# A float32 transformer kernel: the gate and up products of its four SwiGLU layers by seven block products instead of eight, with the down products cut into groups

## The chip, the cores and the metric

The kernel runs on one core of one Trainium2 chip. The metric is the device time of one execution in microseconds (us), the median of several runs. One profiled execution gives the start, duration and engine of every instruction: PE (TensorE, the matmuls; PEld are its weight loads), DVE (VectorE), ACT (ScalarE), POOL (GpSimd), SP (which issues DMAs).

## The reference, cut to what matters

S = 512 tokens, D = 1024 features, D_FF = 2816. Two layers of a first block, each with a SwiGLU before and one after four attention mixers, then a second block that the change doesn't touch.

```python
def swiglu(h, w_gate, w_up, w_down):
    return (jax.nn.silu(h @ w_gate) * (h @ w_up)) @ w_down

for l in range(DEPTH):                                   # DEPTH = 2
    x = x + 0.5 * swiglu(rms_norm(x, ffn1_norm[l]), ffn1_w_gate[l], ffn1_w_up[l], ffn1_w_down[l])
    ...
    x = x + jnp.concatenate([ya, yb, yc, yd], axis=-1) @ w_out[l]
    x = x + 0.5 * swiglu(rms_norm(x, ffn2_norm[l]), ffn2_w_gate[l], ffn2_w_up[l], ffn2_w_down[l])
    x = rms_norm(x, final_norm[l])
```

## The kernel before, in words

Activations lie feature-major: x[k] is a tile of 128 features by 512 tokens, k = 0 to 7. A float32 product is made of three TensorE passes over float32r pairs: each operand is split into a high part (an ACT copy) and a low part (a DVE subtraction), and `mm3` (L98 to L102) multiplies high by high, high by low and low by high. The split activations are xh[k] and xl[k]; the split weights whi and wlo, of which three pairs exist at a time (`weights_`), fed by a DMA into raw, an ACT copy (L89) and a DVE subtraction (L90).

`ffn` is called four times: FFN1 and FFN2 of layer 0, then of layer 1. FFN2 of layer 0 is followed by FFN1 of layer 1 directly; elsewhere the mixers, or the second block, come between. The norm's per-token scale is not in xh and xl: it is a broadcast tile R (`bcast`, L127 and L130), which multiplies the finished gate and up sums, so that the products can begin before the scale is known. `late` (L219 to L222) multiplies x itself by such a scale after FFN2 of layer 0.

`ffn` works in two halves of 11 tiles f, a tile being 128 of the 2816 hidden features. For each f the gate product goes to a PSUM bank s and the up product to a bank t, each 8 k-tiles by three passes = 24 matmuls of 512 columns. Then a = s*R (L245), silu, u = t*R (L249), u*s (L250), and the split of the result into gh[f] and gl[f]. After 11 tiles the half's down products follow: for each of 8 output tiles k, 33 matmuls of 512 columns from gh and gl into a bank acc, then x[k] += 0.5*acc (L270). In the second half done(k) follows each k: `emit_h` makes xh[k] and xl[k] of the next stage (L181, L182) and, by an ACT square (L194) and a POOL addition (L199), the running sum of squares of the next norm.

Each engine runs its instructions in the order the tile scheduler has set; the weights are pulled 100 instructions ahead (`ahead`).

## Time and profile before

| | |
|---|---|
| time, median of 3 runs | 2573.12 us (2571.47 to 2574.28) |
| span of the profiled execution | 2570.1 us |
| PE busy | 2491.1 us, 97%, 12456 matmuls |
| DVE busy | 1353.0 us, 53% |
| ACT busy | 1054.0 us, 41% |
| POOL busy | 517.6 us, 20% |

The profiled execution's own time is its span, 3 us under the median; nothing outside the span is in the records. The four FFNs take 8 to 377, 702 to 1073, 1073 to 1441 and 1767 to 2136 us of it. A matmul's record lasts longer than its distance to the next one, since matmuls are pipelined, so what one matmul costs is the distance from start to start.

### The profile page before, as it was taken

The numbers are of one execution on the slowest core, as the hardware profiler recorded it, in microseconds if no ns is written. First come the engines' busy times: TensorE is split into PE (matmuls) and PEld (weight loads), VectorE is DVE, ScalarE is ACT, GpSimd is POOL, SyncE is SP. The second block draws the span as 40 slices with busy tenths as digits, with TensorE's granted clock in tenths as the row PEclk, the third lists the DMA queues.
The fourth block names the chain that finished last, engine by engine and source line by source line (L and its number), as shares of the span: only waits on it lengthen the run. The fifth ranks groups of instructions, "written<-read, shape, count | busy, mean of one in ns | idle before, by whom it ended". The sixth has DMA issues, their size and how long they took to land.

```text
span 2570.1 us, 32068 instructions
## 1 busy us (share of the span) xinstructions
PE 2491.1 (97%) x12456; PEld 2044.5 (80%) x12456; DVE 1353.0 (53%) x2259; ACT 1054.0 (41%) x1826; POOL 517.6 (20%) x431
## 2 busy tenths in 40 slices
PE   8999999899999999999999999999999999889998
PEld 6888888776688888888888988767888888768867
DVE  6434446976544344454344489755434444854444
ACT  4223236676522233332233476754322334343543
POOL 1000015652200000200000457223000014442312
PEclk9999999999999999999999999999999999989979
DMA  4233243211222322322333332012333334220111
GB/s 154 92 97 99 87 139 100 89 46 38 65 91 86 103 99 86 102 92 86 103 99 102 117 97 81 19 53 84 98 88 103 97 107 134 62 66 30 36 46 56
DMA packets 86137, 220.04 MB, mean 86 GB/s; under 512 B 19088, under 2 KB 22225, under 8 KB 85985
## 3 DMA queue, kind: packets, MB, share of 16 engines
q1 hardware_dynamic: 82576, 217.66, 27.1%
q8 instruction: 98, 1.61, 0.3%
q10 hardware_dynamic: 3408, 0.33, 0.1%
q14 instruction: 55, 0.44, 0.1%
HBM read 209.14 MB, written 8.78 MB: 85 GB/s over the span
## 4 chain that ended last, share of the span: by engine, by line
PE 86%; DVE 10%; ACT 2%; issue 1%; DMA 1%; POOL 0%; SPq 0%; DVEq 0%; POOLq 0%; ACTq 0%
PE acc L100 9%; PE acc L101 9%; PE acc L102 9%; PE s L101 7%; PE s L102 7%; PE s L100 7%; PE t L102 6%; PE t L101 6%; PE t L100 6%; PE acc L314 4%; PE t L461 2%; PE s L421 2%; PE t L514 2%; PE acc L1598 2%; DVE p L434 1%
## 5 line engine op out<-in xcount | busy, mean ns | idle before, releaser
L89 ACT ACTIVATE whi<-raw 128x1024 fp32r<-128x1024 f32 (+4 forms) x415 | 395.2, 953 | 1071.5 <-PE acc L101 349.6
L90 DVE TENSOR_TENSOR wlo<-raw,whi 128x1024 fp32r<-128x1024 f32 (+3 forms) x341 | 369.6, 1084 | 205.3 <-ACT whi L89 204.6
L199 POOL TENSOR_TENSOR sq<-sq,sqt 128x512 f32<-128x512 f32 x59 | 83.4, 1422 | 1395.8 <-issue 1233.6
L100 PE MATMUL s<-xh,whi 128*128 128x512 f32 x736 | 289.1, 393 | 8.5 <-ACT whi L89 8.0
L101 PE MATMUL s<-xl,whi 128*128 128x512 f32 x736 | 289.2, 393 | 5.5 <-DVE xl L182 5.3
L102 PE MATMUL s<-xh,wlo 128*128 128x512 f32 x736 | 287.9, 391 | 0.0
L101 PE MATMUL acc<-gl,whi 128*128 128x512 f32 x704 | 278.1, 395 | 0.0
L102 PE MATMUL acc<-gh,wlo 128*128 128x512 f32 x704 | 278.1, 395 | 0.0
L100 PE MATMUL acc<-gh,whi 128*128 128x512 f32 x704 | 276.8, 395 | 0.0
L101 PE MATMUL t<-xl,whi 128*128 128x512 f32 x704 | 275.0, 391 | 0.0
L100 PE MATMUL t<-xh,whi 128*128 128x512 f32 x704 | 274.6, 390 | 0.0
L102 PE MATMUL t<-xh,wlo 128*128 128x512 f32 x704 | 274.6, 390 | 0.0
L90 POOL TENSOR_TENSOR wlo<-raw,whi 128x1024 fp32r<-128x1024 f32 (+2 forms) x74 | 169.0, 2285 | 204.1 <-ACT whi L89 195.2
L249 DVE TENSOR_TENSOR u<-t,R 128x512 f32<-128x512 f32 x88 | 60.8, 691 | 275.5 <-PE t L102 275.5
L100 PEld LDWEIGHTS s<-xh,whi 128*128 128x128 f32 x736 | 139.2, 189 | 38.1 <-ACT whi L89 8.0
L101 PEld LDWEIGHTS s<-xl,whi 128*128 128x128 f32 x736 | 139.1, 189 | 38.1 <-DVE xl L182 9.6
L314 PE MATMUL acc<-whi,xh 128*128 128x256 f32 (+1 forms) x576 | 167.0, 293 | 2.1 <-DVE gate L1012 1.7
L314 PE MATMUL acc<-wlo,xh 128*128 128x256 f32 (+1 forms) x576 | 168.1, 293 | 0.3 <-DVE wlo L90 0.3
L314 PE MATMUL acc<-whi,xl 128*128 128x256 f32 (+1 forms) x576 | 168.2, 293 | 0.0
L102 PEld LDWEIGHTS s<-xh,wlo 128*128 128x128 f32 x736 | 139.0, 189 | 29.4 <-DVE wlo L90 0.8
L102 PEld LDWEIGHTS acc<-gh,wlo 128*128 128x128 f32 x704 | 132.0, 187 | 32.4
L101 PEld LDWEIGHTS acc<-gl,whi 128*128 128x128 f32 x704 | 131.9, 187 | 32.4
(662 smaller groups left out, 4750.7 us busy)
## 6 DMA issues: line engine op xcount, KB each, us to landing
raw<-in_ffn_gu_dram SPq DMA_DIRECT2D x176, 512.0 KB, 3.4
raw<-in_ffn_d_dram SPq DMA_DIRECT2D x64, 384.0 KB, 3.1
raw<-in_ffn_d_dram SPq DMA_DIRECT2D x64, 320.0 KB, 2.9
raw<-in_w2f_dram SPq DMA_DIRECT2D x25, 512.0 KB, 3.3
xs<-x SPq DMA_DIRECT2D x24, 256.0 KB, 2.0
raw<-in_a_dram SPq DMA_DIRECT2D x12, 512.0 KB, 3.5
x<-xs SPq DMA_DIRECT2D x24, 256.0 KB, 2.9
raw<-in_wo_dram SPq DMA_DIRECT2D x10, 512.0 KB, 4.0
```

The costliest lines, as they stand in the source:

```text
L89: nc.scalar.activation(out=hi, in_=raw, func=AF.Copy)
L90: (lo_eng or self.lo_eng).tensor_tensor(out=lo, in0=raw, in1=hi.bitcast(F32), op=ALU.subtract)
L100: mm(out=out, lhsT=lh, rhs=rh, start=start, stop=False)
L101: mm(out=out, lhsT=lh, rhs=rl, start=False, stop=False)
L102: mm(out=out, lhsT=ll, rhs=rh, start=False, stop=stop)
L199: nc.gpsimd.tensor_tensor(out=acc, in0=acc, in1=q, op=ALU.add)
L249: nc.vector.tensor_tensor(out=u, in0=prods[1], in1=R, op=ALU.mult)
L314: mm = lambda l, r, st=False, sp=False: nc.tensor.matmul(out=ps[i], lhsT=l, rhs=r, start=st, stop=sp, skip_group_check=True)
L421: nc.tensor.matmul(out=o, lhsT=q[:, i * P:(i + 1) * P], rhs=k[:, keys], start=(n == 0), stop=(n == len(pairs) - 1))
L461: nc.tensor.matmul(out=ps[r, a:z], lhsT=v[:, j, c0:c0 + 64], rhs=pts[j][:, a:z], start=(m == 0), stop=(m == n - 1), skip_group_check=True)
L514: nc.tensor.transpose(ps[:, i * P:(i + 1) * P], probs[i][:, o:o + P], b.ident)
L1598: mm = lambda i, l, r, st=False: nc.tensor.matmul(out=ps[i], lhsT=l, rhs=r, start=st, stop=False, skip_group_check=True)
```

## The change: seven block products, and down products in groups

Tiles f = 0 to 2 (`DIRECT = 3`) are made as before (`direct`). For f = 3 to 21 gate and up together are taken as one product of blocks: the weights as [[gate k 0-3, gate k 4-7], [up k 0-3, up k 4-7]], the activations as [[k 0-3, tokens 0-255 and 256-511], [k 4-7, the same]], and Winograd's form of Strassen's method makes it with seven block products where there are eight. Each block product is 4 k-tiles by three passes = 12 matmuls of 256 columns, so a tile takes 84 matmuls of 256 columns instead of 48 of 512.

The activations' seven forms are made once per FFN by `forms`, from x, the norm's gain and R, so they wait for R: for each of 4 k, two scale operations on DVE, four subtractions of 256 columns on POOL, four ACT copies and four DVE subtractions give fh[k] and fl[k]. They stand behind tile f = 0 in the program. The weights' forms are made for each f by `blocks`: four DMAs of 256 KB into the slots of xh and xl (which are free once the direct tiles are done; the tile f = 3 borrows slots of gh and gl), two sums on POOL and two on DVE of 128x512, seven ACT copies and seven DVE subtractions into four whi/wlo pairs. `winograd` runs the products and joins them with one ACT copy and five DVE additions of 256 columns. The multiplications by R (two of 128x512) and the split of 128x1024 weights fall away for these tiles.

The down products are cut into groups of 4, 4, 4, 4, 3 and 3 tiles f (`CHUNKS`). Those of one group are issued among the next group's gate and up, two k at a time (three in part of the groups of three); x[k] is updated 6 times per FFN. Only the last group of three tiles leaves its eight down products of 9 matmuls, with done(k), at the end of the FFN. In FFN2 of layer 1 the last update goes through a temporary tile and an ACT copy. 

```diff
-HALF = NFF // 2
...
+    def direct(self, gp, wgu, f, R):
+        nc = self.nc
+        prods = []
+        for which in range(2):
+            wh, wl = self.weights(wgu[f, which], (KT, P))
+            ps = self.bank("st"[which], 3)
+            for k in range(KT):
+                self.mm3(ps, wh[:, k], wl[:, k], self.xh[k], self.xl[k], k == 0, k == KT - 1)
+            prods.append(ps)
+        s = self.t(gp, "s")
+        nc.vector.tensor_tensor(out=s, in0=prods[0], in1=R, op=ALU.mult)
+        nc.scalar.activation(out=s, in_=s, func=AF.Silu)
+        u = self.t(gp, "cu")
+        nc.vector.tensor_tensor(out=u, in0=prods[1], in1=R, op=ALU.mult)
+        return u, s
+    def forms(self, gp, gain, R):
+        nc = self.nc
+        out = []
+        for k in range(4):
+            hs = []
+            for j, tag in ((k, "gh3"), (k + 4, "gl3")):
+                h = self.t(gp, tag)
+                nc.vector.scalar_tensor_tensor(out=h, in0=self.x[j], scalar=gain[:, j:j + 1], in1=R, op0=ALU.mult, op1=ALU.mult)
+                hs.append(h)
+            a, b = hs
+            H, L = self.t(gp, f"fh{k}", (P, 7, 256), F32R), self.t(gp, f"fl{k}", (P, 7, 256), F32R)
+            half = lambda t: t.rearrange("p (e c) -> p e c", e=2)
+            w0, w1 = half(self.t(gp, "cu")), half(self.t(gp, "s"))
+            lo, hi = slice(0, 256), slice(256, 512)
+            sub = lambda o, x, y: nc.gpsimd.tensor_tensor(out=o, in0=x, in1=y, op=ALU.subtract)
+            sub(w0[:, 0], a[:, hi], a[:, lo])
+            sub(w0[:, 1], b[:, hi], w0[:, 0])
+            sub(w1[:, 0], b[:, hi], a[:, hi])
+            sub(w1[:, 1], b[:, lo], w0[:, 1])
+            for j, src in ((0, half(a)[:, 0:1]), (1, half(b)), (3, w0), (5, w1)):
+                n = src.shape[1]
+                nc.scalar.activation(out=H[:, j:j + n], in_=src, func=AF.Copy)
+                nc.vector.tensor_tensor(out=L[:, j:j + n], in0=src, in1=H[:, j:j + n].bitcast(F32), op=ALU.subtract)
+            out.append((H, L))
+        return out
+    def blocks(self, gp, wgu, f):
+        nc = self.nc
+        with self.tc.high_priority(offset=self.ahead):
+            if f == DIRECT:
+                slots = [(gp, f"g{t}{4 + i}") for t in "hl" for i in range(4)]
+            else:
+                slots = [(self.xp, f"x{t}{4 * (f % 2) + i}") for t in "hl" for i in range(4)]
+            slot = iter(slots)
+            A = []
+            for which in range(2):
+                for e in range(2):
+                    t = self.t(*next(slot))
+                    nc.sync.dma_start(out=t, in_=wgu[f, which][:, e * S:(e + 1) * S])
+                    A.append(t)
+            a11, a12, a21, a22 = A
+            s1, s2, s3, s4 = (self.t(*next(slot)) for _ in range(4))
+            for eng, o, x, y, op in ((nc.gpsimd, s1, a21, a22, ALU.add), (nc.vector, s2, s1, a11, ALU.subtract),
+                                     (nc.gpsimd, s3, a11, a21, ALU.subtract), (nc.vector, s4, a12, s2, ALU.subtract)):
+                eng.tensor_tensor(out=o, in0=x, in1=y, op=op)
+            out = []
+            for pair in ((a11, s2), (s1, s3), (a12, s4), (a22,)):
+                hi = self.wp.tile([P, 1024], F32R, tag="whi", name=self.name("whi"), bufs=3)
+                lo = self.wp.tile([P, 1024], F32R, tag="wlo", name=self.name("wlo"), bufs=3)
+                for e, src in enumerate(pair):
+                    c = slice(e * S, (e + 1) * S)
+                    nc.scalar.activation(out=hi[:, c], in_=src, func=AF.Copy)
+                    nc.vector.tensor_tensor(out=lo[:, c], in0=src, in1=hi[:, c].bitcast(F32), op=ALU.subtract)
+                    v = lambda t: t[:, c].rearrange("p (k m) -> p k m", k=4)
+                    out.append((v(hi), v(lo)))
+        return out
+    def winograd(self, gp, wgu, f, F):
+        nc = self.nc
+        a11, s2, s1, s3, a12, s4, a22 = self.blocks(gp, wgu, f)
+        pa, pb = self.bank("s", 3), self.bank("t", 3)
+        lo, hi = slice(0, 256), slice(256, 512)
+        def prod(out, w, j, start=False, stop=False):
+            wh, wl = w
+            for k in range(4):
+                H, L = F[k]
+                for n, (x, y) in enumerate(((wh, H), (wh, L), (wl, H))):
+                    nc.tensor.matmul(out=out, lhsT=x[:, k], rhs=y[:, j], start=start and k == 0 and n == 0, stop=stop and k == 3 and n == 2,
+                                     skip_group_check=True)
+        add = lambda o, x, y: nc.vector.tensor_tensor(out=o, in0=x, in1=y, op=ALU.add)
+        prod(pa[:, lo], a11, 0, start=True)
+        prod(pa[:, hi], s2, 4)
+        t, U2, V = (self.t(gp, n, (P, 256)) for n in ("w6", "wu", "wv"))
+        u, s = self.t(gp, "cu"), self.t(gp, "s")
+        nc.scalar.activation(out=t, in_=pa[:, hi], func=AF.Copy)
+        add(U2, pa[:, lo], t)
+        prod(pb[:, lo], s1, 3, start=True)
+        prod(pb[:, hi], s3, 5)
+        add(V, pb[:, lo], U2)
+        add(u[:, hi], pb[:, hi], V)
+        prod(pa[:, lo], a12, 1, stop=True)
+        nc.scalar.activation(out=s[:, lo], in_=pa[:, lo], func=AF.Silu)
+        prod(pb[:, lo], s4, 2)
+        add(s[:, hi], pb[:, lo], U2)
+        nc.scalar.activation(out=s[:, hi], in_=s[:, hi], func=AF.Silu)
+        prod(pb[:, hi], a22, 6, stop=True)
+        add(u[:, lo], pb[:, hi], U2)
+        return u, s
+    def ffn(self, r, wgu, wd, gain, done, reorder=False):
         nc = self.nc
         with self.tc.tile_pool(name=self.name("ffn"), bufs=1, reuse_waits="tile") as gp:
             R = self.bcast(r, gp, "R", ACC)
-            self.late()
-            for half in range(2):
-                gh, gl = [], []
-                for f in range(HALF):
-                    prods = []
-                    for which in range(2):
-                        wh, wl = self.weights(wgu[half * HALF + f, which], (KT, P))
-                        ps = self.bank("st"[which], 3)
-                        for k in range(KT):
-                            self.mm3(ps, wh[:, k], wl[:, k], self.xh[k], self.xl[k], k == 0, k == KT - 1)
-                        prods.append(ps)
-                    a = self.t(gp, "a")
-                    nc.vector.tensor_tensor(out=a, in0=prods[0], in1=R, op=ALU.mult)
-                    s = self.t(gp, "s")
-                    nc.scalar.activation(out=s, in_=a, func=AF.Silu)
-                    u = self.t(gp, "u")
-                    nc.vector.tensor_tensor(out=u, in0=prods[1], in1=R, op=ALU.mult)
-                    nc.vector.tensor_tensor(out=u, in0=u, in1=s, op=ALU.mult)
-                    h = self.t(gp, f"gh{f}", dt=F32R)
-                    l = self.t(gp, f"gl{f}", dt=F32R)
-                    nc.scalar.activation(out=h, in_=u, func=AF.Copy)
-                    nc.vector.tensor_tensor(out=l, in0=u, in1=h.bitcast(F32), op=ALU.subtract)
-                    gh.append(h)
-                    gl.append(l)
-                if half == 1:
-                    self.new_h()
-                for k in range(KT):
-                    ps = self.bank("acc", 2)
-                    for f0, f1 in ((0, 6), (6, HALF)):
-                        wh, wl = self.weights(wd[half, k][:, f0 * P:f1 * P], (f1 - f0, P))
-                        for f in range(f0, f1):
-                            self.mm3(ps, wh[:, f - f0], wl[:, f - f0], gh[f], gl[f], f == 0, f == HALF - 1)
-                    old, new = self.x[k], self.x[k]
-                    if reorder:
-                        new = self.x[k] = self.t(gp, f"xa{k}") if half == 0 else self.t(self.xp, f"x{k}")
-                    v = (lambda a: a.rearrange("p (c r) -> p r c", r=8)) if reorder and half else (lambda a: a)
-                    o = new.rearrange("p (r c) -> p r c", r=8) if reorder and half else new
-                    nc.vector.scalar_tensor_tensor(out=o, in0=v(ps), scalar=0.5, in1=v(old), op0=ALU.mult, op1=ALU.add)
-                    if half == 1:
-                        done(k)
+            F = None
+            def up(f, i):
+                u, s = self.direct(gp, wgu, f, R) if f < DIRECT else self.winograd(gp, wgu, f, F)
+                nc.vector.tensor_tensor(out=u, in0=u, in1=s, op=ALU.mult)
+                h = self.t(gp, f"gh{i}", dt=F32R)
+                l = self.t(gp, f"gl{i}", dt=F32R)
+                nc.scalar.activation(out=h, in_=u, func=AF.Copy)
+                nc.vector.tensor_tensor(out=l, in0=u, in1=h.bitcast(F32), op=ALU.subtract)
+                return h, l
+            def down(k, f0, f1, g):
+                ps = self.bank("acc", 2)
+                wh, wl = self.weights(wd[k][:, f0 * P:f1 * P], (f1 - f0, P))
+                for j, (h, l) in enumerate(g):
+                    self.mm3(ps, wh[:, j], wl[:, j], h, l, j == 0, j == f1 - f0 - 1)
+                x = self.x[k]
+                if reorder and f1 == NFF:
+                    t = self.t(gp, "R" if k % 2 else "xa")
+                    v = lambda a: a.rearrange("p (c r) -> p r c", r=8)
+                    nc.vector.scalar_tensor_tensor(out=t.rearrange("p (r c) -> p r c", r=8), in0=v(ps), scalar=0.5, in1=v(x), op0=ALU.mult, op1=ALU.add)
+                    nc.scalar.activation(out=x, in_=t, func=AF.Copy)
+                else:
+                    nc.vector.scalar_tensor_tensor(out=x, in0=ps, scalar=0.5, in1=x, op0=ALU.mult, op1=ALU.add)
+            downs = []
+            for n, (f0, f1) in enumerate(zip(CHUNKS, CHUNKS[1:])):
+                g = []
+                for f in range(f0, f1):
+                    g.append(up(f, 4 * (n % 2) + f - f0))
+                    if F is None:
+                        F = self.forms(gp, gain, R)
+                        self.late()
+                    for _ in range(-(-len(downs) // (f1 - f))):
+                        downs.pop(0)()
+                downs = [lambda k=k, f0=f0, f1=f1, g=g: down(k, f0, f1, g) for k in range(KT)]
+            self.new_h()
+            for k in range(KT):
+                downs[k]()
+                done(k)
+CHUNKS = (0, 4, 8, 12, 16, 19, NFF)
+DIRECT = 3
...
-        b.ffn(r, A[f"ffn1_gu{l}"], A[f"ffn1_d{l}"], done_mix)
+        b.ffn(r, A[f"ffn1_gu{l}"], A[f"ffn1_d{l}"], g["ffn1_g", 0] if l == 0 else g["next", 0], done_mix)
-        b.ffn(r, A[f"ffn2_gu{l}"], A[f"ffn2_d{l}"], lambda k: b.emit_h(k, gn, g["fin_g", l]), l == 1)
+        b.ffn(r, A[f"ffn2_gu{l}"], A[f"ffn2_d{l}"], g["ffn2_g", l], lambda k: b.emit_h(k, gn, g["fin_g", l]), l == 1)
...
-            w[f + "_d"] = np.stack([feat_units(d[:HALF * P]), feat_units(d[HALF * P:])], 0)
+            w[f + "_d"] = feat_units(d)
```

How instructions move, at three places.

TensorE in the first FFN, from the last pass of tile f = 2 to tile f = 3; s and t are PSUM banks, fh0 and fl0 the forms of k = 0, whi and wlo the weights. Before:

```order
L102 MATMUL t_87_394<-xh7_31_143,wlo_86_391 128x512
L100 MATMUL s_96_436<-xh0_3_81,whi_94_432 128x512
L101 MATMUL s_96_436<-xl0_4_82,whi_94_432 128x512
L102 MATMUL s_96_436<-xh0_3_81,wlo_95_433 128x512
L100 MATMUL s_96_436<-xh1_7_89,whi_94_432 128x512
```

After:

```order
L101 MATMUL t_109_472<-xh7_31_143,wlo_108_469 128x512
L317 MATMUL s_130_545<-fh0_68_287,whi_122_523 128x256
L317 MATMUL s_130_545<-fl0_69_288,whi_122_523 128x256
L317 MATMUL s_130_545<-fh0_68_287,wlo_123_524 128x256
L317 MATMUL t_131_546<-fh0_68_287,whi_124_529 128x256
L317 MATMUL s_130_545<-fh1_74_307,whi_122_523 128x256
```

Where tile f = 3 needed only what the stage before had left, xh and xl, it now needs the forms, which R and a chain on DVE, POOL and ACT precede. In the first FFN 52 direct matmuls stand behind the broadcast of R on this engine, in the others 84, 66 and 84.

GpSimd in the first FFN, behind the norm's scale rs4. Before, nothing of the FFN's inside runs there, and the next norm's sums follow:

```order
L119 TENSOR_TENSOR rs4_50_199<-ms_49_197,neghalf_72 128x4
L199 TENSOR_TENSOR sq_405_2244<-sq_405_2244,sqt_415_2298 128x512
L199 TENSOR_TENSOR sq_405_2244<-sq_405_2244,sqt_425_2353 128x512
L199 TENSOR_TENSOR sq_405_2244<-sq_405_2244,sqt_435_2408 128x512
L199 TENSOR_TENSOR sq_405_2244<-sq_405_2244,sqt_445_2463 128x512
```

After, from the last subtraction of the forms of k = 1 on; xl2, xl0, xl6 and xl4 are block sums for f = 4 and f = 5, cu and s hold the forms of k = 2 and 3:

```order
L260 TENSOR_TENSOR s_77_310<-gl3_73_305,cu_76_309 128x256
L292 TENSOR_TENSOR xl2_145_659<-xh0_139_649,xh2_141_653 128x512
L292 TENSOR_TENSOR xl0_143_657<-xh2_141_653,xh3_142_655 128x512
L260 TENSOR_TENSOR cu_82_329<-gh3_78_323 128x256
L292 TENSOR_TENSOR xl6_178_841<-xh4_172_831,xh6_174_835 128x512
L260 TENSOR_TENSOR s_83_330<-gl3_79_325,gh3_78_323 128x256
L292 TENSOR_TENSOR xl4_176_839<-xh6_174_835,xh7_175_837 128x512
L260 TENSOR_TENSOR cu_82_329<-gl3_79_325,cu_82_329 128x256
L260 TENSOR_TENSOR cu_88_349<-gh3_84_343 128x256
L260 TENSOR_TENSOR s_83_330<-gl3_79_325,cu_82_329 128x256
L260 TENSOR_TENSOR cu_88_349<-gl3_85_345,cu_88_349 128x256
L260 TENSOR_TENSOR s_89_350<-gl3_85_345,gh3_84_343 128x256
```

Four block sums, whose inputs are loaded into slots that the direct tiles still read, now stand ahead of seven of the eight subtractions for k = 2 and 3.

VectorE in a steady tile of the first FFN. Before, tile f = 5; a and u are the gate and up sums, R the broadcast scale:

```order
L245 TENSOR_TENSOR a_127_638<-s_122_582,R_53_209 128x512
L90 TENSOR_TENSOR wlo_138_683<-raw_136_680,whi_137_682 128x1024
L249 TENSOR_TENSOR u_129_642<-t_126_613,R_53_209 128x512
L250 TENSOR_TENSOR u_129_642<-u_129_642,s_128_640 128x512
L90 TENSOR_TENSOR wlo_147_725<-raw_145_722,whi_146_724 128x1024
L254 TENSOR_TENSOR gl5_131_646<-u_129_642,gh5_130_645 128x512
```

After, twelve rows in tile f = 7, from its first addition on; xl5 and xl7 are block sums, x6 a residual tile that takes a down product:

```order
L320 TENSOR_TENSOR wu_257_1260<-s_254_1233,w6_256_1259 128x256
L320 TENSOR_TENSOR wv_258_1261<-t_255_1234,wu_257_1260 128x256
L320 TENSOR_TENSOR cu_259_1262<-t_255_1234,wv_258_1261 128x256
L89 TENSOR_TENSOR wlo_266_1341<-raw_264_1338,whi_265_1340 128x512
L292 TENSOR_TENSOR xl5_309_1568<-xl4_308_1567,xh4_304_1559 128x512
L292 TENSOR_TENSOR xl7_311_1570<-xh5_305_1561,xl5_309_1568 128x512
L320 TENSOR_TENSOR s_260_1263<-t_255_1234,wu_257_1260 128x256
L89 TENSOR_TENSOR wlo_270_1361<-raw_268_1358,whi_269_1360 128x512
L370 SCALAR_TENSOR_TENSOR x6_26_132<-acc_263_1337,x6_26_132 128x512
L300 TENSOR_TENSOR wlo_280_1394<-xh0_271_1377,whi_279_1393 128x512
L300 TENSOR_TENSOR wlo_280_1394<-xl1_276_1386,whi_279_1393 128x512
L320 TENSOR_TENSOR cu_259_1262<-t_255_1234,wu_257_1260 128x256
```

Six rows per tile became twenty, and the block sums, the weights' splits and the additions that drain PSUM stand in one row on this engine.

## Rows read from the trace of the kernel before

**Rows 1.** The page: busy time, the chain by engine, a group with mean ns.
```profile
PE 2491.1 (97%) x12456; PEld 2044.5 (80%) x12456; DVE 1353.0 (53%) x2259; ACT 1054.0 (41%) x1826; POOL 517.6 (20%) x431
...
PE 86%; DVE 10%; ACT 2%; issue 1%; DMA 1%; POOL 0%; SPq 0%; DVEq 0%; POOLq 0%; ACTq 0%
...
L89 ACT ACTIVATE whi<-raw 128x1024 fp32r<-128x1024 f32 (+4 forms) x415 | 395.2, 953 | 1071.5 <-PE acc L101 349.6
```
**Rows 2.** Stretches of two FFNs: PE, PEld, DVE, ACT, POOL busy, clock, DMA share, GB/s.
```profile
135.00:377.00 242.00, 242.00 (x1054) 197.33 (x1053) 100.71 (x122) 70.57 (x91) 8.58 (x6) 1.00 0.33 104
...
1092.00:1260.00 168.00, 168.00 (x735) 137.56 (x734) 75.90 (x96) 46.29 (x58) 0.00 (x0) 1.00 0.31 93
```
**Rows 3.** Timeline of PE, 200 to 240 us: first and last of 178 gate/up matmuls.
```profile
199.72 0.39 PE L100 MATMUL s<-xh,whi 128*128 128x512 f32 x1
...
239.84 0.39 PE L100 MATMUL s<-xh,whi 128*128 128x512 f32 x1
```
**Rows 4.** Timeline of PE, 320 to 360 us: first and last of 173 down matmuls.
```profile
319.76 0.40 PE L101 MATMUL acc<-gl,whi 128*128 128x512 f32 x1
...
359.89 0.40 PE L102 MATMUL acc<-gh,wlo 128*128 128x512 f32 x1
```
**Rows 5.** The chain of waits: start, us; two runs of 256-column matmuls (L314, stationary xh).
```profile
377.09 6.12 PE acc L314 x51
...
384.10 16.93 PE acc L314 x141
```
**Rows 6.** Timeline of PE and DVE, FFN2 of layer 0: its first matmul, and R's copy.
```profile
702.54 0.50 PE L100 MATMUL s<-xh,whi 128*128 128x512 f32 x1 [0.24 <-ACT xh L181]
...
723.95 0.69 DVE L130 COPY R<-acc 128x512 f32<-128x512 f32 x1 [0.61 <-PE acc L127]
```
**Rows 7.** Timeline of DVE, 1091 to 1100 us: back-to-back operations of 128x512.
```profile
1091.44 0.69 DVE L245 TENSOR_TENSOR a<-s,R 128x512 f32<-128x512 f32 x1
1092.04 0.68 DVE L249 TENSOR_TENSOR u<-t,R 128x512 f32<-128x512 f32 x1
...
1093.84 5.39 DVE L221 SCALAR_TENSOR_TENSOR x<-x,fin_g,sqt 128x512 f32<-128x512 f32 x8
```
**Rows 8.** Groups by line with busy us, mean ns: POOL at 256 and 512 columns.
```profile
L199 POOL TENSOR_TENSOR sq<-sq,sqt 128x512 f32<-128x512 f32 x59 | 83.4, 1422 | 1395.8 <-issue 1233.6 <-ACT sqt L194 161.8
...
L362 POOL TENSOR_TENSOR dup<-x,ahr 128x256 f32<-128x256 f32 x32 | 20.5, 672 | 69.8 <-PE t L390 69.8
```
**Rows 9.** The page's DMA issues: KB each, us from issue to landing.
```profile
x<-xs SPq DMA_DIRECT2D x24, 256.0 KB, 2.9
```
**Rows 10.** Timeline of PE, 702 to 713 us: a stall, and the two matmuls' distance behind it.
```profile
705.89 0.80 PE L101 MATMUL s<-xl,whi 128*128 128x512 f32 x1 [2.62 <-DVE xl L182]
706.49 0.63 PE L102 MATMUL s<-xh,wlo 128*128 128x512 f32 x1
...
711.18 0.63 PE L100 MATMUL s<-xh,whi 128*128 128x512 f32 x1
711.61 0.49 PE L101 MATMUL s<-xl,whi 128*128 128x512 f32 x1
```
**Rows 11.** Timeline of DVE and POOL, end of FFN2 of layer 0, from one down product's drain.
```profile
1057.59 0.69 DVE L270 SCALAR_TENSOR_TENSOR x<-acc,x 128x512 f32<-128x512 f32 x1 [2.13 <-PE acc L102]
1059.16 0.74 DVE L182 SCALAR_TENSOR_TENSOR xl<-x,gnext,xh 128x512 fp32r<-128x512 f32 x1
...
1059.64 2.68 POOL L199 TENSOR_TENSOR sq<-sq,sqt 128x512 f32<-128x512 f32 x2 [5.03 <-ACT sqt L194]
...
1065.29 0.69 DVE L270 SCALAR_TENSOR_TENSOR x<-acc,x 128x512 f32<-128x512 f32 x1 [2.13 <-PE acc L102]
```
**Rows 12.** Timeline of DVE and POOL at the kernel's start, both busy side by side.
```profile
10.15 9.86 POOL L199 TENSOR_TENSOR sq<-sq,sqt 128x512 f32<-128x512 f32 x6 [9.71 <-ACT sqt L194]
10.31 10.27 DVE L182 SCALAR_TENSOR_TENSOR xl<-x,ffn_g,xh 128x512 fp32r<-128x512 f32 x6
```

More of the change, by code (lines that the diff above doesn't have):

```diff
@@ L58, in load @@
         return t
-    BUFS = dict(sqt=2, ms=4, hms=4, rs4=4, rs8=2, r12=2, a=2, s=2, u=2, nm=6, sum=6, rsum=6, cms=2, lms=2, lats=2,
+    BUFS = dict(sqt=2, ms=4, hms=4, rs4=4, rs8=2, r12=2, s=2, cu=2, wu=2, nm=6, sum=6, rsum=6, cms=2, lms=2, lats=2,
                 beta=2, sq_=1, st=10, p=8, pth=3, ptl=3, vv=2, lat=6, ysq=2, c1=4, sums=3, frs=2, ft=2, fR=2, rr=1, y=4, dup=4, bias=1,
@@ L225, in post_norm @@
         return r
-    def ffn(self, r, wgu, wd, done, reorder=False):
+    def direct(self, gp, wgu, f, R):
[13 more added lines that the diff above has]
+        return u, s
```

## The prediction

> **What bounds the kernel now.** The page first: PE is busy 97% of the span and the chain that ends last is 86% PE, with DVE next at 53% busy [rows 1]. Then the FFN stretches, where all of the change lies: PE is busy for every one of the 242 and 168 us shown, at full clock, DVE for 42 to 45%, POOL hardly or not at all [rows 2]. So the FFNs are bound by PE alone, and a matmul saved there is time saved until another engine's chain takes over. Then the distance from start to start: 0.2267 us for a gate or up matmul (40.12 us over 177 steps) [rows 3] and 0.2333 for a down matmul (40.13 over 172) [rows 4]. For 256 columns the trace has the runs of the mixers' L314: 6.12 us over 51 and 16.93 over 141, both 0.1200 [rows 5].
>
> **The gate and up products.** A tile costs 48 x 0.2267 = 10.88 us now. After, it costs 84 matmuls of 256 columns, 21,504 columns in place of 24,576, but with 84 starts in place of 48. Their price lies between two rows. L314's 0.1200 [rows 5] gives 10.08 us, a gain of 0.80 per tile. But at 512 columns the trace has two prices for the same shape, and what differs is the moving tile: xh and xl at 0.2267, gh and gl, which lie in the FFN's own pool, at 0.2333, a step of 0.0067. The forms fh and fl lie in that same pool, so I add the step: 0.1200 + 0.0067 = 0.1267, 10.64 us, a gain of 0.24 per tile. There are 4 x 19 = 76 such tiles: 18 us by 0.1267, 61 us by 0.1200. I take **18**, as gh is nearer to fh in where it lies. The down products stay 528 of 512 columns per FFN, from gh and gl: 0.
>
> A Trainium skill page speaks for more: "TensorE: Matmul & The Clock Gate" (section "Wait — 56ns, not 53.3ns?") gives a warm matmul N / 2.4 GHz plus about 2.5 ns from start to start. That is 215.8 ns at 512 columns and 109.2 at 256, and by it the gain would be, as an estimate, 48 x 0.2158 - 84 x 0.1092 = 1.19 us per tile, 90 us in all. The trace disagrees: 0.2267 and 0.1200 are each about 13 ns over N / 2.4 [rows 3, 5].
>
> **The forms.** Before, R is needed only to drain the banks. Now it starts a chain that the fourth tile waits for. In FFN2 of layer 0 R is copied 21.4 us after the first product [rows 6], while the three direct tiles last 144 x 0.2267 = 32.6 us. In the built order 52, 84, 66 and 84 direct matmuls stand behind the broadcast of R in the four FFNs: 11.8, 19.0, 15.0 and 19.0 us of cover. From R to the last fl DVE has 40, 41, 49 and 41 instructions. Back to back they start 0.60 us apart, the scale operations with two tensors and a column 0.66 (L221: eight in 5.39) [rows 7]. Each list has 8 scale operations (16 in FFN1 of layer 1, where `late` adds 8) and 4 additions of 256 columns, put at half; with one 1024-column split in the FFN2s that is 23.4, 24.5, 29.3 and 24.5 us. Less the cover: 11.6, 5.5, 14.3 and 5.5, together 37. A low end: some 34 block-product matmuls of k = 0 and 1 can run in each FFN while the rest arrives, 34 x 0.1267 = 4.3 us, so 20 in all. I credit no such filling, because in the FFN1s POOL stands in the way. There the sums for f = 4 and 5 stand ahead of seven subtractions for k = 2 and 3, and their loads wait until the direct tiles have read xh and xl: after the last direct matmul come a DMA of 2.9 us [rows 9], two sums of 1.42 and seven subtractions of 0.67 [rows 8], 10.4 us, which agrees with 11.6 and 14.3 and no less. A high end: if DVE waits out every POOL operation that runs meanwhile, 16 x 0.67 + 4 x 1.42 = 16.4 us more per FFN, of which some is idle already; I put 61 for the four.
>
> Each stall also costs clock. After a stall of 2.62 us TensorE's matmuls start 0.43 us apart, the 1.2 GHz level, from 706.49 to 711.61: 12 steps at 0.427 where 0.2267 would do, 2.4 us [rows 10]. Four stalls: 9. Forms in all: 37 + 9 = **46**, ends 20 and 70.
>
> **The tails.** The last half's eight downs took 7.70 us each (1057.59 to 1065.29) [rows 11], 33 matmuls, which hid everything that done(k) does. Now they are 9 matmuls, 9 x 0.2333 = 2.10 us. Per k POOL has 2.68 us [rows 11], so the sum of squares ends about 8 x (2.68 - 2.10) = 4.6 us later against PE than it did, and R with it. DVE has 0.69 for x and 0.74 for xl [rows 11] and about 0.6 for a weight split, 2.0 us, just under 2.10; but beside a busy POOL six xl took 10.27 us, 1.71 each [rows 12], which makes it 3.0 and 0.9 late per k. The next stage takes its k in order at 0.68 each (three passes), so it feels between nothing and 4 us. Four FFNs: 0 to 16, I take **8**. The copy through ACT in the last FFN hides behind those same matmuls.
>
> **Steady tiles (f = 5 on).** PE needs 84 x 0.1267 + 24 x 0.2333 = 16.2 us per tile. DVE has 20 instructions, at 0.60 at most 12.0. ACT has 13, at the 0.953 of mostly larger copies [rows 1] at most 12.4. POOL has two sums, 2.84. All are under 16.2, so PE keeps the end, but the orders are tight: whi and wlo have three buffers for six weights per tile, so the next tile's first pair waits for this tile's seventh product, with only 10 down matmuls, 2.3 us, to cover one ACT copy and one DVE subtraction (1.2 us) and whatever those two engines have in hand. Before, no such wait shows [rows 2]. Bounds: nothing, or the 0.7 us of one operation in hand at each of 68 tiles, 48. I take one in eight, about 5, and 1 us for the last group in each FFN, where the gl of tile 21 is late for its own down products: **9**.
>
> **Sum.** 2570.1 - 18 + 46 + 8 + 9 = 2615 for a profiled execution. The median stood 3 us above the span, so **2618**.
>
> **Rivals.** (1) The cheap matmul: the 0.0067 step is not the pool's, and the block products run at L314's 0.1200. For it: the only row at 256 columns. Against: gh. It gives 43 us back: 2575, and this is the case on the other side, faster once the other terms stay under 56 us where I have 63. (2) The forms are hidden: the scheduler's cover holds, R comes early, and the low end of 20 minus the clock decides; 2618 - 37 = 2581 at 0.1267, and 2538 with the cheap matmul. Against: R at 21.4 us of 32.6. (3) POOL locks DVE in every tile. In rows 12 a DVE operation with two SBUF inputs, 0.74 alone [rows 11], lasts as long as the POOL operation beside it. In a steady tile POOL's 2.84 us, each sum of which can hold such a DVE operation, would come on top of 12.0, and both sums head the chain of the weight splits; if 0.6 us per tile then shows on PE, 76 x 0.6 = 46: 2664.
>
> The Trainium skill, "SBUF — State Buffer" (section "Who interferes with whom"), has this as an exclusive lock on a port pair that DVE and GpSimd share. The pairs of rows 12 agree with it, 1.71 us against 0.74.
>
> (4) The price goes by columns alone: half of 0.2267 for 256, 0.1133. Then a tile costs 9.52 us, the gain is 1.36 per tile, 103 in all: 2533. Against: L314's 0.1200 [rows 5]; no row of this kernel shows it.
>
> The page named above comes nearest to that; by its own 90 us the sum would be 2546.
>
> **Chances.** My own sum 0.50, the cheap matmul 0.24, hidden forms 0.10, the lock 0.13, a price by columns alone 0.03. My sum's own range, by the bounds of its terms, is 2592 to 2650. Eight in ten must leave out the cheapest combination (cheap matmul with hidden forms) and the far end of the lock: 2552 to 2662. About 0.2%, 5 us, is what a measurement of this kernel can tell from no change. Faster: half of the cheap matmul, half of the hidden forms, and the price by columns: 0.20. Within: a third of the cheap matmul: 0.08. Slower: the rest, 0.72.
>
> **What would show it.** In the profile after: the distance from start to start of L317 matmuls in a steady tile (0.1267, or 0.1200); an idle gap on PE ahead of L317 at the start of f = 3 in each FFN, with DVE fl or ACT fh as its releaser, 5 to 15 us, and half clock behind it; PE busy without gaps from f = 5 on, with 16.2 us per tile (15.7 in rival 1); POOL's L260 rows of k = 2 and 3 starting after the direct tiles' end in the FFN1s; DVE's subtractions L300 at 0.69 (over 1.2 beside L292 if the lock rules). The prediction is wrong if PE has no gap at f = 3, or gaps in every tile.

## The result, and the profile after

The changed kernel takes 2590.04 us (median of 5 runs, 2586.50 to 2595.99) against 2571.47 (5 runs, 2561.88 to 2574.28). The ratio on record is 1.0102, 95% interval 1.0073 to 1.0131, which is 26 us; the two medians by themselves are 19 us apart (1.0072), and the profiled execution spans 2588.3 us, 18 more than before's. So the change is slower, as forecast, by 18 to 26 us instead of the forecast 45 (from 2573), and the time lies inside the range.

The page of the changed kernel, its busy line and one of its groups (busy us, mean ns, idle before and its releaser):

```profile
PE 2438.3 (94%) x15192; PEld 2114.6 (82%) x15192; DVE 1877.3 (73%) x3307; ACT 1293.1 (50%) x2494; POOL 814.9 (31%) x647
...
L317 PE MATMUL s<-fl,whi 128*128 128x256 f32 x912 | 258.9, 284 | 26.6 <-DVE fl L268 26.6
```

PE is busy 53 us less than in [rows 1] and yet the span is 18 us longer: its idle time went from 79 to 150 us. The stretches of the first FFN say where (PE, PEld, DVE, ACT, POOL busy, granted clock, DMA share, GB/s): direct tiles, the first two block tiles (f = 3, 4), the other 17, the end.

```profile
8.50:46.90 38.40, 38.22 (x161) 29.24 (x160) 34.00 (x43) 20.29 (x34) 21.38 (x16) 1.00 0.57 173
46.90:95.00 48.10, 32.66 (x194) 28.63 (x193) 44.73 (x62) 20.51 (x39) 20.42 (x17) 0.75 0.23 69
95.00:363.00 268.00, 268.00 (x1863) 247.95 (x1862) 202.36 (x344) 119.64 (x222) 43.81 (x30) 1.00 0.32 93
363.00:382.00 19.00, 17.58 (x73) 12.71 (x71) 16.12 (x23) 11.77 (x20) 6.97 (x5) 1.00 0.63 189
```

The 17 tiles run without a gap at full clock, as the FFN did in [rows 2]. The two before them take 48.10 us where their 168 block-product and 24 down matmuls need 25.2 (prices below), at a mean clock of 0.75. The same stretch in the other FFNs:

```profile
750.00:790.60 40.60, 30.21 (x194) 28.01 (x193) 38.10 (x55) 18.47 (x36) 17.29 (x14) 0.79 0.27 85
1117.70:1166.50 48.80, 31.11 (x194) 27.06 (x193) 45.81 (x64) 19.84 (x38) 17.79 (x15) 0.79 0.21 67
1823.10:1863.50 40.40, 29.89 (x194) 27.41 (x193) 39.22 (x56) 18.61 (x36) 15.86 (x13) 0.83 0.27 86
```

That is 177.9 us, 77 over 4 x 25.2. PE is idle for 15.4, 10.4, 17.7 and 10.5 us of the four, 54 in all; the other 23 us are matmuls that run slower, at half clock.

The price of a block product, from PE's timeline (start, duration; between these rows 60 matmuls run in one piece):

```profile
282.59 0.28 PE L317 MATMUL s<-fh,whi 128*128 128x256 f32 x1
...
289.59 0.40 PE L99 MATMUL acc<-gh,whi 128*128 128x512 f32 x1
```

7.00 us over 60 is 0.1167, half of the 0.2333 of [rows 4], and less than both prices that the prediction's sum weighed. A tile's 84 cost 9.80 us, 1.08 less than its 10.88 by [rows 3]: 82 us over 76 tiles.

PE's waits at the first block tile, in brackets with what ended them, and what DVE and POOL did meanwhile:

```profile
50.34 0.39 PE L317 MATMUL s<-fl,whi 128*128 128x256 f32 x1 [1.50 <-DVE fl L268]
53.70 0.58 PE L317 MATMUL t<-fl,whi 128*128 128x256 f32 x1 [2.79 <-DVE fl L268]
60.36 0.58 PE L317 MATMUL s<-fl,whi 128*128 128x256 f32 x1 [4.97 <-DVE fl L268]
```
```profile
42.84 0.68 DVE L268 TENSOR_TENSOR fl<-gl,fh 128x512 fp32r<-128x512 f32 x1
...
50.21 1.76 DVE L268 TENSOR_TENSOR fl<-gl,fh 128x512 fp32r<-128x512 f32 x1
51.90 1.75 DVE L268 TENSOR_TENSOR fl<-cu,fh 128x512 fp32r<-128x512 f32 x1
```
```profile
39.16 1.18 POOL L260 TENSOR_TENSOR s<-gl,gh 128x256 f32<-128x256 f32 x1
...
49.97 3.12 POOL L292 TENSOR_TENSOR xl<-xh,xh 128x512 f32<-128x512 f32 x2
```

PE waits for fl, and DVE, which makes it, is never idle from R at 35.26 to the last fl at 71.65. The same subtraction takes 0.68 us alone and 1.75 beside a POOL sum, and POOL's own subtraction 1.18 where 256 columns took 0.67 in [rows 8].

The Trainium skill, "SBUF — State Buffer" (section "Who interferes with whom"), gives the reason as one port pair that DVE and GpSimd can only hold in turn; 0.68 against 1.75 agrees.

### The profile page after: what moved, and what is told of

It is laid out like the page before. It is cut to its first block, busy times and chain, and to the rows that moved or that the text cites. A ratio compares the mean times of both kernels' runs of the same rounds, so it can differ in the third digit from the quotient of the medians.

```text
span 2588.3 us, 40395 instructions
## 1 busy us (share of the span) xinstructions
PE 2438.3 (94%) x15192; PEld 2114.6 (82%) x15192; DVE 1877.3 (73%) x3307; ACT 1293.1 (50%) x2494; POOL 814.9 (31%) x647
## 5 line engine op out<-in xcount | busy, mean ns | idle before, releaser
L88 ACT ACTIVATE whi<-raw 128x512 fp32r<-128x512 f32 (+4 forms) x327 | 246.1, 754 | 433.5 <-PE t L317 222.4
L317 PE MATMUL t<-fl,whi 128*128 128x256 f32 x1216 | 342.6, 282 | 8.8 <-DVE fl L268 8.8
L317 PE MATMUL t<-fh,whi 128*128 128x256 f32 x1216 | 342.5, 282 | 6.2 <-ACT fh L267 6.2
L317 PE MATMUL t<-fh,wlo 128*128 128x256 f32 x1216 | 342.3, 281 | 1.0 <-DVE wlo L300 1.0
L317 PE MATMUL s<-fl,whi 128*128 128x256 f32 x912 | 258.9, 284 | 26.6 <-DVE fl L268 26.6
L317 PE MATMUL s<-fh,whi 128*128 128x256 f32 x912 | 259.0, 284 | 11.4 <-ACT fh L267 8.4
L317 PE MATMUL s<-fh,wlo 128*128 128x256 f32 x912 | 257.1, 282 | 0.2 <-DVE wlo L300 0.2
L317 PEld LDWEIGHTS t<-fl,whi 128*128 128x128 f32 x1216 | 231.4, 190 | 16.1 <-DVE fl L268 9.8
L317 PEld LDWEIGHTS t<-fh,whi 128*128 128x128 f32 x1216 | 231.1, 190 | 13.5 <-ACT fh L267 7.0
L317 PEld LDWEIGHTS t<-fh,wlo 128*128 128x128 f32 x1216 | 231.5, 190 | 1.4 <-DVE wlo L300 1.4
```

Of the source, the lines that this page charges most:

```text
L88: nc.scalar.activation(out=hi, in_=raw, func=AF.Copy)
L317: nc.tensor.matmul(out=out, lhsT=x[:, k], rhs=y[:, j], start=start and k == 0 and n == 0, stop=stop and k == 3 and n == 2, skip_group_chec ...
```

## The experiments

Each ratio is to the kernel before, run on the same chip beside it (median 2560.5 to 2561.5 there, so ratios are compared, not times). The changed kernel was not run again beside them, so a difference from its 1.0102 carries both intervals, about 0.3% (8 us) each way.

**What the forms cost.** The body of `forms` but for its tiles is replaced.

```diff
-            hs = []
...
+            for o in (H, L):
+                nc.gpsimd.memset(o.bitcast(F32), 1.0)
             out.append((H, L))
```

> The activations' forms are not made: their tiles are filled with a constant by eight POOL memsets per FFN, so the block products multiply constants; everything else is as in the changed kernel. Theory (the forms eat what the block products save): in the profile after, the stretch from the first block product to the start of tile f = 5 lasts 48.1, 40.5, 48.8 and 40.3 us, where two tiles at 0.1167 us per block product and 24 down matmuls of 0.2333 need 25.2; so 77 us go with the forms and the kernel takes 2590 - 77 = 2513 us (2505 to 2520). Rival (the loss lies in the cut down products, their tails, or the loads of the blocks): 2550 or more, and the stretch stays over 30 us.

Measured: 0.9858 (0.983 to 0.9886), 2527 us. The stretch of the first two block tiles, here in two of the FFNs:

```profile
728.20:760.20 32.00, 28.15 (x194) 26.56 (x193) 25.57 (x39) 12.39 (x24) 9.39 (x6) 0.89 0.35 108
1086.60:1123.90 37.30, 28.20 (x193) 26.02 (x193) 33.74 (x54) 15.31 (x29) 6.50 (x6) 0.91 0.26 82
```

The four are 31.9, 32.0, 37.3 and 31.1 us, 132 where the changed kernel has 178: the forms cost 46 us there, and 1.0102 - 0.9858 = 62 us in the whole time. The two profiled executions are 64 us apart: 48 of them lie in the FFNs, 6 in the mixers and 10 behind the last FFN, where neither the forms nor the change reach. 31 of the 77 us remain without the forms. In FFN2 of layer 0 PE waits for DVE's first addition, and DVE is held up by POOL's sums for f = 4 and 5, whose loads end with the direct tiles (PE, then DVE, then POOL):

```profile
737.81 0.58 PE L301 MATMUL s<-fh,whi 128*128 128x256 f32 x1 [3.85 <-DVE wu L304]
```
```profile
730.46 1.78 DVE L334 TENSOR_TENSOR cu<-cu,s 128x512 f32<-128x512 f32 x1
```
```profile
728.70 2.99 POOL L276 TENSOR_TENSOR xl<-xh,xh 128x512 f32<-128x512 f32 x2 [18.80 <-DMA xh<-in_ffn_gu_dram]
```

In FFN1 of layer 1, the longest of the four, `late` adds its eight operations on DVE, 6.5 us, ahead of the same addition. So the theory was right on the place and too simple on the cause: the loads and sums of the blocks, which its rival named, have their share.

**Whether POOL is to blame.** The forms' subtractions move to DVE.

```diff
-            sub = lambda o, x, y: nc.gpsimd.tensor_tensor(out=o, in0=x, in1=y, op=ALU.subtract)
+            sub = lambda o, x, y: nc.vector.tensor_tensor(out=o, in0=x, in1=y, op=ALU.subtract)
```

> The 16 subtractions per FFN of the forms go from POOL to DVE, nothing else. Theory (POOL and DVE hold each other up): in the changed kernel DVE takes 36.4 us from R to the last fl in the first FFN where its 40 instructions back to back need 23.4, with subtractions of 1.2 and 1.75 us beside POOL instead of 0.68; with the subtractions on DVE it has 16 x 0.33 = 5.3 us more and no such neighbour: about 29 to 31, 5 us saved in each FFN: 2570 us (2560 to 2580). Rival (DVE's own list is the limit, contention or not): 5.3 us more per FFN: 2611 us.

Measured: 1.0079 (1.0054 to 1.0104). The same stretch, and the moved subtraction (min, median, max ns):

```profile
46.30:92.20 45.90, 32.03 (x193) 28.55 (x192) 42.45 (x70) 20.72 (x39) 9.11 (x6) 0.78 0.22 71
748.10:789.00 40.90, 31.54 (x194) 28.27 (x193) 35.61 (x59) 17.44 (x33) 9.19 (x6) 0.83 0.28 87
```
```profile
L260 DVE TENSOR_TENSOR cu<-gh x16: 410/418/427, 39.8 to 1828.6; 128x256 f32<-128x256 f32 x16
```

175 us instead of 178 in the four: both numbers missed. DVE operations of over 1 us between R and the last fl fall from 15 to 4 in the first FFN, so the holding up is real, but the 16 subtractions take its place on DVE, and the chain goes from 36.4 to 35.2 us only. DVE is full either way: with the subtractions on DVE the forms are bound by DVE's list.

**What cover is worth.** One direct tile more.

```diff
-DIRECT = 3
+DIRECT = 4
```

> DIRECT = 4 instead of 3. Theory (the forms are late for want of cover): the stretch from the first block product to two tiles later was 16.2, 8.6, 11.5 and 9.3 us longer with forms than without, 46 us in all; one more direct tile per FFN covers 10.9 us and costs 10.88 - 84 x 0.1167 = 1.08, so about 40 - 4 = 36 us come back: 0.996 of the time of the kernel before. Rival (the sums of the tiles f = DIRECT + 1 and + 2, which wait until the direct tiles are done, hold the forms up wherever the direct tiles end): the same loss plus 4 us, 1.010 or more.

Measured: 0.9983 (0.9964 to 1.0002), 30 us better than the changed kernel where 36 were expected. Two stretches of the first two block tiles, which now need 30.8 us, as both carry 24 down matmuls:

```profile
62.70:103.80 41.10, 35.24 (x216) 31.70 (x217) 36.26 (x56) 18.20 (x34) 10.29 (x7) 0.88 0.24 71
754.70:796.10 41.40, 35.14 (x217) 31.82 (x216) 34.33 (x54) 17.74 (x33) 8.47 (x6) 0.92 0.33 97
```

The four lose 41 us instead of 77, so 36 came back there, less 4 for the direct tiles. Its rival, the same loss plus 4 us, is ruled out; that the sums have a part in the 41 that are left is not.

**What the cut of the down products costs.** All gate and up products direct, no forms; then the same with a longer last group.

```diff
-DIRECT = 3
+DIRECT = 22
...
-                    if F is None:
-                        F = self.forms(gp, gain, R)
-                        self.late()
+                    if f == 0:
+                        self.late()
```

> DIRECT = 22 and no forms: all gate and up products as before the change, but the down products in groups among them. Theory: this leaves only the price of the cut down products, which is the tails: the FFNs' ends lie 18.5 to 21 us behind the last gate or up product where eight products of 9 matmuls need 16.8, and the next stage starts a few us late: 2575 to 2585 us. Rival (the cut costs as much as the net loss of the change): 2590 or more. Rival (the cut gives time back): under 2569.

Measured: 1.0082 (1.0051 to 1.0113): 21 us, more than the theory had and as much as the first rival had, near the net loss of the whole change. The profiled execution shows 10 us of them up to the end of the last FFN (2145.7 against 2135.6). PE waits for drains in the FFNs' ends, which it never does there in the kernel before, and behind the last FFN for a weight split (the last line):

```profile
1072.93 0.47 PE L99 MATMUL acc<-gh,whi 128*128 128x512 f32 x1 [1.24 <-DVE x L370]
```
```profile
2143.81 0.47 PE L99 MATMUL acc<-gh,whi 128*128 128x512 f32 x1 [1.61 <-DVE R L367]
2149.01 0.50 PE L101 MATMUL acc<-xh,wlo 128*128 128x512 f32 x1 [2.32 <-DVE wlo L89]
```

```diff
-CHUNKS = (0, 4, 8, 12, 16, 19, NFF)
+CHUNKS = (0, 4, 7, 10, 14, 18, NFF)
```

> As direct22 (all gate and up products direct, no forms), with groups of 4, 3, 3, 4, 4 and 4 tiles, so that the last eight down products have 12 matmuls, 2.80 us, where they had 9, 2.10. Theory (the price of the cut is its short tail, in which POOL's 2.68 us per k for the sums of squares and DVE's share no longer fit): direct22's 1.0082 comes down to about 1.004. Rival (the price lies in the cut itself, 48 drains and 48 weight loads per FFN where there were 16 of each): 1.008 stays.

Measured: 1.0002 (0.9983 to 1.0021). So the price is the short tail, and by the ratio the cut itself is free; in the profiled executions 7 of the 10 us go (2145.7 against 2138.4 at the end of the last FFN) and 3 stay. The medians are 19 us apart. The profiled execution of direct22 is the shortest of its four (2575.4 us, the others 2583.7 to 2585.6) and that of direct22_tail4 the longest of its ten (2556.5 to 2569.1), so 7 is the low end; where the rest lies no trace shows.

**Where the sums of the first block tile stand.** In the changed kernel PE waits in the output projection ahead of FFN2; PE, then DVE, then POOL:

```profile
705.19 0.50 PE L99 MATMUL acc<-xh,whi 128*128 128x512 f32 x1 [1.94 <-DVE x L1003]
```
```profile
702.79 1.74 DVE L292 TENSOR_TENSOR gl<-gl,gh 128x512 f32<-128x512 f32 x1 [1.19 <-POOL gl L292]
704.46 0.68 DVE L1003 TENSOR_TENSOR x<-acc,x 128x512 f32<-128x512 f32 x1
```
```profile
701.01 1.75 POOL L292 TENSOR_TENSOR gl<-gh,gh 128x512 f32<-128x512 f32 x1
```

The block sum of tile f = 3, pulled ahead into the mixers' end, waits for POOL, and the drain that PE needs stands behind it.

```diff
-                eng.tensor_tensor(out=o, in0=x, in1=y, op=op)
+                (nc.gpsimd if f == DIRECT else eng).tensor_tensor(out=o, in0=x, in1=y, op=op)
```

> For tile f = 3 all four block sums run on POOL, where two ran on DVE. Theory: in the changed kernel the two on DVE, pulled ahead into the end of the mixers, wait there for POOL's sums with the drains of the output projection queued behind them, and the stretch from the end of FFN1 to FFN2's first product lasts 329.8 and 330.4 us where it lasted 325.6 and 326.1; it comes back to within 1.5 us of that, and the time to about 1.0075 of the kernel before. Rival (POOL, longer busy, makes the sum of squares and so R later by what is gained): 1.010, with the stretch shorter and the forms' stall longer.

Measured: 1.0082 (1.0053 to 1.0111), not to be told from 1.0102. In the profile the wait is 0.34 us, but the FFN's first product now waits:

```profile
704.84 0.50 PE L99 MATMUL acc<-xh,whi 128*128 128x512 f32 x1 [0.34 <-DVE x L1003]
710.04 0.50 PE L99 MATMUL s<-xh,whi 128*128 128x512 f32 x1 [1.85 <-ACT xh L180]
```

From the end of FFN1 to FFN2's first product it takes 329.4 us (330.1 in the changed kernel, 325.8 in the kernel before); in layer 1 it is 328.1 (330.6, 326.3). So 3.2 of the 8.6 us come back in the two layers. The rival came true as well: the stretch of the first two block tiles is longer behind it, 42.3, 51.4 and 42.2 us in the second, third and fourth FFN where the changed kernel has 40.6, 48.8 and 40.4, 6 us in all:

```profile
1117.60:1169.00 51.40, 34.65 (x193) 30.71 (x192) 45.81 (x64) 19.68 (x37) 17.63 (x15) 0.70 0.20 64
```

The mechanism is shown; its cure is none.

**What a matmul's price hangs on.** 32 bytes ahead of the FFN's pool, in the changed kernel and in the kernel before.

```diff
+            gp.tile([P, 8], F32, tag="pad", name=self.name("pad"), bufs=1)
             R = self.bcast(r, gp, "R", ACC)
```

> A tile of 32 bytes per partition is put ahead of the FFN's pool, so that gh, gl, fh and fl start 32 bytes past a multiple of 64, as xh and xl do; nothing else. Theory (a matmul's price per column hangs on where its moving tile starts): down matmuls go from 0.2333 to 0.2267 us and block-product matmuls from 0.1167 to 0.1133, 2112 x 0.0067 + 6384 x 0.0033 = 35 us: 2555 us. Rival (the place doesn't matter): 0.2333 and 0.1167 stay, 2590 us.

Measured: 1.0040 (1.0020 to 1.0061), 16 us better than the changed kernel, half of the 35 expected. Sixty block products of it:

```profile
976.95 0.28 PE L317 MATMUL s<-fh,whi 128*128 128x256 f32 x1
...
983.75 0.39 PE L99 MATMUL acc<-gh,whi 128*128 128x512 f32 x1
```

6.80 / 60 = 0.1133, the price expected, in three of the FFNs for most of them (0.1145 to 0.1151 on average there); in the first FFN they stay at 0.1174 on average.

> The kernel before with a tile of 32 bytes ahead of the FFN's pool, so that gh and gl start where xh and xl do against a multiple of 64 bytes. Theory (the price per column hangs on the start of the moving tile): its down matmuls go from 0.2333 to between 0.2293, as with the same tile in the changed kernel, and 0.2267, 2112 x 0.004 to 0.0067 = 8 to 14 us: 0.9945 to 0.997 of the kernel before. Rival (the changed kernel's gain came from elsewhere): 1.000.

Measured: 0.9967 (0.9948 to 0.9985). The first and the last of 176 down matmuls:

```profile
319.70 0.39 PE L100 MATMUL acc<-gh,whi 128*128 128x512 f32 x1
...
359.98 0.39 PE L102 MATMUL acc<-gh,wlo 128*128 128x512 f32 x1
```

40.28 / 175 = 0.2302 instead of 0.2333 (0.2290 on average over all down products). So the place is a part of the price, but not all of it.

**Versions that beat both.**

> DIRECT = 4, the 32 bytes ahead of the FFN's pool, and the first block tile's sums on POOL, together in the changed kernel. Theory: the three don't overlap; 1.0102 - 0.014 (cover) - 0.006 (place) - 0.0025 (sums) = 0.988 of the kernel before. Rival (with the forms covered, the stalls that are left all come from the block sums and the cut downs): 0.995 or more.

Measured: 0.9935 (0.9916 to 0.9954), 2544 us, between the theory and its rival; the first tile's sums had shown no gain clear of noise. About 0.003 of it are the 32 bytes, which the kernel before can have too (0.9967).

> d4_pad_pool with the groups of direct22_tail4. Theory (short tail): 2 to 4 us per FFN's end come back, 0.9935 goes to about 0.990. Rival (no price in the tail): 0.9935.

Measured: 0.9961 (0.9945 to 0.9977), no better. In the first FFN f = 4 and 5 take 45.9 us instead of 40.9, but only because they carry 72 down matmuls instead of 48, which is 5.5 us. What is new are waits in the tiles f = 7 to 13, 16 us in the four FFNs: with groups of three tiles a block tile carries mostly 18 or 27 down matmuls, and PE waits there for the weights of the down products.

```profile
152.41 0.50 PE L101 MATMUL acc<-gh,wlo 128*128 128x512 f32 x1 [1.06 <-DVE wlo L89]
```

A tile with 18 of them needs about 14 us of PE and takes about 15. So the steady tiles have little slack: the longer tail pays only where the groups behind it stay long.

> d4_pad_pool with DIRECT = 5; tile f = 5 takes six free slots of gh and gl and two new ones for its blocks. With DIRECT = 4 the two tiles behind the direct ones still take 41 us where 31 would do. Theory A (what is left is the rest of the forms' chain): one more direct tile takes away most of these 10 us at a price of 1.1 per FFN: 0.980. Theory B (what is left is the block sums and loads of tiles DIRECT + 1 and + 2, which start when the direct tiles end, wherever that is, as the 31.9 us of no_forms say): the 10 us stay and the price of one more direct tile is paid: 0.995.

Measured: 0.9890 (0.9861 to 0.9919), 2530.5 us, the best here. Two stretches behind the direct tiles:

```profile
79.60:112.70 33.10, 31.03 (x217) 28.62 (x217) 26.53 (x45) 14.49 (x27) 3.82 (x3) 1.00 0.26 80
759.10:795.10 36.00, 32.52 (x218) 30.10 (x217) 27.81 (x45) 14.07 (x26) 6.86 (x5) 0.95 0.32 98
```

Between the two theories: the four lose 21 us now where d4_pad_pool loses 42, so one more direct tile took away half of what was left, and the clock is back at 0.91 to 1.00. The last fl is now made before the direct tiles end in all four FFNs (65.2 us against 79.6 in the first). That DVE then has room for the block sums too is argued, not shown.

```diff
-                (nc.gpsimd if f == DIRECT else eng).tensor_tensor(out=o, in0=x, in1=y, op=op)
+                (nc.gpsimd if f == DIRECT else nc.vector).tensor_tensor(out=o, in0=x, in1=y, op=op)
```

> d5_pad_pool with the two POOL sums of every block tile but the first on DVE as well. In d5_pad_pool the two tiles behind the direct ones take 33.1, 36.0, 38.8 and 35.9 us, 20.6 us more than 4 x 30.8. Theory (what is left there are POOL's sums of the next tiles, beside which DVE's operations take 1.2 to 1.8 us instead of 0.7): half or more of it goes, with no stall in the steady tiles, where DVE has 2 x 0.6 us more of 15.4: 0.985 of the kernel before. Rival (DVE's list is the limit there, with or without POOL): the stretches stay or grow, 0.989 or more.

Measured: 0.9888 (0.9856 to 0.9920), the same time. The stretches are 32.1, 37.0, 34.2 and 36.8 us: 4 of the 20.6 us went, so POOL's sums are not most of what is left there. Its block products, at the same place as in d5_pad_pool, cost this:

```profile
954.51 0.28 PE L317 MATMUL s<-fh,whi 128*128 128x256 f32 x1
...
961.58 0.40 PE L99 MATMUL acc<-gh,whi 128*128 128x512 f32 x1
```

7.07 / 60 = 0.1178, against 0.1133 in pad_after with the same 32 bytes. Over the steady tiles the average is 0.1167 to 0.1178 in the four FFNs here and 0.1145 to 0.1173 in d5_pad_pool, which takes back 8 us (945.8 us against 937.7 for those tiles). So the equal time doesn't say what the move itself was worth, and what sets the price besides the place stays open.

## Why the prediction was right, and where its steps were not

The sign and the range were right by luck: two terms were both too small, with opposite signs. With the gain as measured and the other terms as forecast the sum would have been 2570 - 82 + 63 = 2551, faster, and the sign wrong. The prediction's own range, 2592 to 2650, leaves the measured time just outside; it took the low end of the forms but not those of the tails and the steady tiles, with which it would have begun at 2575.

- **Gate and up products: -18 forecast, -82 measured.** The step that failed is "0.1200 + 0.0067". It took the excess over the columns for a fixed cost per matmul and added what differed at 512 columns to a row at 256. In the changed kernel the excess goes with the columns: 0.1167 is 0.2333 / 2. The nearest row was gh's, as the prediction said; it had to be halved, not added to. Rival (4), with a chance of 0.03, halved too, but the wrong row (0.2267). Halving is no rule for all kernels: in d5_sums_dve block products of 0.1178 stand beside down matmuls of 0.2294.
- **Forms: +46 forecast, ends 20 and 70; +77 measured in the stretch.** Gap, place, releaser and half clock came as described: waits of up to 4.97 us for fl, clock 0.75 to 0.83. Both parts were too small: 37 us of waiting were forecast and 54 came, and 9 us of half clock (four stalls of 2.4, rightly 9.6) where 23 came. The forms alone are 46 (no_forms), but that this is the forecast's number is luck: DVE took 36.4, 37.7, 41.5 and 37.5 us from R to the last fl instead of 23.4, 24.5, 29.3 and 24.5, since its operations beside POOL took up to 1.76 us. The sum had that only in its high end. It credited no filling because POOL's sums would wait for their loads; in the first FFN POOL goes from the forms of k = 1 to the first two sums without a pause (49.97) and afterwards waits for DVE. Nor do four sums stand ahead of seven subtractions there: two stand ahead of all eight, the third ahead of seven, the fourth ahead of six. The other 31 are missing from the sum: the first block tile starts while POOL makes the sums of the next two, even with the forms there.
- **Tails: +8 forecast, 0 to 16.** direct22 less direct22_tail4 says 7 in the profiled executions and 19 in the medians, the latter beyond the range. One reading was wrong: the 2.68 us of POOL in [rows 11] are two additions, for the two norms behind FFN2. The ends of the FFN1s have one:

```profile
348.44 1.35 POOL L199 TENSOR_TENSOR sq<-sq,sqt 128x512 f32<-128x512 f32 x1 [6.35 <-ACT sqt L194]
```

There POOL fits into 2.10 us. The sum also left out that PE itself waits for the drain, as two acc banks cover only 2 x 2.10 us.
- **Steady tiles: +9 forecast, 0 measured**: PE busy 268.00 of 268.00 us. The three weight buffers suffice, and rival (3), the lock in every tile, does not reach PE there: POOL's 44 us lie beside DVE's 202 and PE never waits. That holds for these groups only; with 18 down matmuls per tile it does wait (d4_tail4).
- **Not in the sum:** the first block tile's sums, pulled ahead into the mixers, 4.3 us in each layer between FFN1 and FFN2 (330.1 against 325.8, 330.6 against 326.3), of which about 1 is there without them too (direct22: 326.5 and 327.4).

Added up, with 8 for the tails: -82 + 77 + 8 + 0 + 8 = 11 of the 18 us between the two spans; 7 us are not assigned, of which 1 lies behind the last FFN. Rival (2), hidden forms, is what the experiments made true: with two more direct tiles, the 32 bytes and the first sums on POOL it is 0.9890. The 32 bytes alone take the kernel before to 0.9967, so about 0.8% is left for the change; two more direct tiles alone were not run, and one more alone, 0.9983, is not told from the kernel before.

## What to carry to other kernels

An algorithm with fewer multiplications gives its gain in the steady state and takes its price at the start: ask what the first tile now waits for, count that chain at the durations it has beside the other engines' work, and cover it with tiles done in the old way. What is pulled ahead lands in another stage's in-order queues, and an end that was long enough to hide the next stage's preparation has to stay that long. To price a matmul of another width, look at whether the excess over the columns goes with the columns, scale the row whose operands lie most alike, and keep a range around it. And when two large terms of opposite sign decide, ask what the sign would be if only one of them were wrong.

## What was not expected of the hardware

A matmul from start to start took 0.2267, 0.2302 or 0.2333 us at 512 columns and 0.1133, 0.1167, 0.1178 or 0.1200 at 256, in long runs without a wait at full clock; moving the tiles by 32 bytes changed it by 1.3% (0.2333 to 0.2302) and, in most FFNs, by up to 3% (0.1167 to 0.1133). 0.3% of the whole kernel before hangs on those 32 bytes.

The Trainium skill, "TensorE: Matmul & The Clock Gate" (section "Wait — 56ns, not 53.3ns?"), has one fixed excess of about 2.5 ns; the runs show 6.6 to 13.3 ns at 256 columns and 13.3 to 20 at 512, so the measurement decides: it is larger, it moves with the tiles' place, and in gh and fh of the changed kernel it doubles with the columns.
